# Feed-forward products of an encoder layer as seven block products, in two passes

## The chip, the core and the metric

One core of a Trainium2 chip runs the kernel. The metric is the device time of one execution in microseconds. The kernel before takes 2031.93 us, the median of three runs (2030.33 to 2033.82).

## What is computed

One layer of a streaming encoder in float32, on 1024 prompt tokens and 32 sample tokens (T = 1056 tokens together, width 1024): two recurrent mixers, a projection, cross-attention over a memory, a feed-forward part, a final normalisation. The change lies in the feed-forward part:

```python
D_FF = 2816
...
n = rmsnorm(x, lw['norm_ffn'])
x = x + (jax.nn.silu(n @ lw['w_ff1']) * (n @ lw['w_ff3'])) @ lw['w_ff2']
...
y = rmsnorm(x, norm_final)
```

## The kernel before

**Recording and order.** The network is not issued as it is written. Every call of an engine becomes a node of a graph; `Graph.order` then places the nodes engine by engine with a price for each operation (`price`, L209), gives each tile a place in SBUF or a PSUM bank for as long as its nodes need it, and `Graph.emit` issues them in that order. The line that all instructions carry in the profile is that of `emit` (L337). Each engine works its queue in the order so fixed; all DMAs go through SyncE's queue. `nc.bias` shifts a node's urgency, `nc.phase` and `LEAD` say from when nodes of a later part may be placed, `FIFO` limits how many tiles of a class live at once, and `HOME` says in which region of SBUF a class may lie (`REGIONS`, in units of 66 words of a partition; `f0` has 192 of them).

**Matrix products.** A float32 operand is split into two float32r parts, high and low: ScalarE casts (`CAST`), VectorE or GpSimd subtracts. A product is then three matmuls, high by high, high by low and low by high. `load_w` (L718) loads a column tile of a weight, 128 columns, multiplies it by the norm's gain on VectorE and splits it. `gemm` (L732) goes over three blocks of 352 tokens; the weights are the stationary operand:

```python
for t0, n in blocks:
    ps = self.psg.tile([128, 512], F32, tag="g", name="ps_g")[:, :n]
    for i, k in enumerate(ks or range(nk)):
        ...
        nc.tensor.matmul(ps, lhsT=hi[:, k], rhs=ah, start=i == 0, stop=False)
        ...
        nc.tensor.matmul(ps, lhsT=hi[:, k], rhs=al, start=False, stop=False)
        nc.tensor.matmul(ps, lhsT=lo[:, k], rhs=ah, start=False, stop=i == nk - 1)
    evac(t0, n, ps)
```

**The feed-forward part** (`ffn`, L993). `x` stays in SBUF in its two parts (`xh`, `xl`) and is the moving operand as it is; the factor 1/rms of each token (`rb`, from `rstd`, L884) is multiplied in when a product is taken out of PSUM, so the first products need no `rb`. `hidden(m)` makes one tile of 128 inner features (22 in all): eight input tiles by three blocks for `w_ff1`, the same for `w_ff3`, then sigmoid and products, and the split. After 6, 6, 6, 2 and 2 such tiles (`FF_GROUPS`) `ff2` multiplies that group by its rows of `w_ff2` and adds into the accumulators `acc`, so the inner activations never leave SBUF. The last group goes by blocks of 512, 288 and 256 tokens (`LAST`), so that `final` (transposes on TensorE, squares on ScalarE, `rstd_pow` on GpSimd, a scaling on VectorE, the store) can begin on the first tokens while the last are multiplied.

That is 4752 matmuls of the feed-forward part: 3168 for `w_ff1` and `w_ff3` and 1440 for `w_ff2`, all of 352 tokens, and 48 each of 512, 288 and 256.

**The step ahead of it.** `w_co` of the cross-attention is the last product before the feed-forward part. `residual` (L862) takes it out of PSUM: two additions on VectorE, a cast on ScalarE and a subtraction on GpSimd for the new `x`, and its squares (ScalarE, GpSimd), from which `rstd` gets `rb` over a ones-matmul, Ln, Exp and a Newton step on VectorE.

## Time and profile before

| | |
|---|---|
| median of three runs | 2031.93 us |
| profiled execution: span from first to last instruction | 2034.7 us (no other time is listed for it) |
| TensorE matmuls busy | 1954.2 us, 96% of the span |
| VectorE, ScalarE, GpSimd busy | 1101.1, 801.0, 622.5 us |
| DMA | 100.59 MB, mean 49 GB/s |
| mean granted TensorE clock | 0.978 |

The profile is one execution. PE is TensorE's matmuls, PEld its weight loads (they overlap), DVE is VectorE, ACT ScalarE, POOL GpSimd, SP SyncE. In a group's row stand the engine, the operation, written and read tiles, the shape, the count, then the busy time in us and the mean of one in ns, then idle time ahead of it and what ended that. In a row of the timeline stand the start in us, the length in us, engine, operation, tiles, shape and count; neighbours of one kind are merged. Tiles bear the names of their SBUF regions (`f`, `r`, `mb`, `ma`, `wr`) or `bank` for PSUM. A row of the windows has for each engine the busy time in the stretch, then the granted clock, the DMA engines' busy share and GB/s.

### The profile page before, as it was taken

How to read it: one execution, taken by the hardware profiler on the slowest of the kernel's cores; microseconds unless marked ns; L12 is line 12 of the kernel's file. 1: busy time of each engine (PE TensorE's matmuls, PEld its weight loads, DVE VectorE, ACT ScalarE, POOL GpSimd, SP SyncE). 2: the span in 40 equal slices, each digit the busy share in tenths (PEclk: the TensorE clock that was granted, in tenths of full speed). 3: DMA queues.
4: the chain of work that ended last, by engine and by line, in shares of the span. 5: the costliest groups of instructions: out<-in, count | busy, mean ns of one | idle time of the engine just before them, and what ended most of it. 6: DMA issues, size and time to landing. Idle time of an engine off the chain costs nothing.

```text
span 2034.7 us, 36538 instructions
## 1 busy us (share of the span) xinstructions
PE 1954.2 (96%) x14417; PEld 1813.2 (89%) x14417; DVE 1101.1 (54%) x2584; ACT 801.0 (39%) x2066; POOL 622.5 (31%) x954
## 2 busy tenths in 40 slices
PE   7989999998999899899999999999999999999998
PEld 6878777787877788899989999999999999999997
DVE  4876677768767766635754356333333344323345
ACT  4576546845765676633332233121111112111122
POOL 4742343334434331206300056230022233310221
PEclk8999999998999999899999999999999999999999
DMA  4100100011010101541211111111211111111112
GB/s 139 42 22 25 35 23 27 23 34 33 22 32 18 33 23 58 179 147 42 73 42 42 42 53 42 42 40 40 59 50 39 40 58 42 50 40 53 46 42 86
DMA packets 159115, 100.59 MB, mean 49 GB/s; under 512 B 7776, under 2 KB 153824, under 8 KB 158944
## 3 DMA queue, kind: packets, MB, share of 16 engines
q1 hardware_dynamic: 158944, 98.26, 16.0%
q8 instruction: 113, 1.85, 0.4%
q14 instruction: 58, 0.48, 0.1%
HBM read 86.69 MB, written 11.55 MB: 48 GB/s over the span
## 4 chain that ended last, share of the span: by engine, by line
PE 59%; DVE 4%; POOL 1%; ACT 1%; issue 1%; DMA 1%; SPq 0%; DVEq 0%; ACTq 0%
PE bank L337 59%; DVE f L337 2%; ACT f L337 1%; POOL f L337 1%; DVE r L337 1%; POOL r L337 1%; DVE mb L337 0%; ACT mb L337 0%; DMA wr<-in_w_ck_dram 0%; ACT r L337 0%; DMA f<-mix_scratch 0%; DMA wr<-in_w_cq_dram 0%; DVE wr L337 0%; SPq L337 0%; POOL mb L337 0%
## 5 line engine op out<-in xcount | busy, mean ns | idle before, releaser
L337 PE MATMUL bank<-r 128*128 128x352 f32 x5904 | 1040.1, 331 | 12.4 <-POOL r L337 5.3
L337 PEld LDWEIGHTS bank<-r 128*128 128x128 f32 x5904 | 955.1, 190 | 27.6 <-POOL r L337 5.8
L337 DVE TENSOR_TENSOR f<-bank,f 128x256 f16<-128x256 f32 (+9 forms) x689 | 252.6, 391 | 355.4 <-PE bank L337 339.8
L337 PE MATMUL bank<-mb,r 128*128 128x352 f32 (+3 forms) x2448 | 411.5, 325 | 4.6 <-DVE r L337 2.5
L337 PEld LDWEIGHTS bank<-mb,r 128*128 128x128 f32 x2448 | 396.1, 188 | 9.5 <-DVE r L337 4.3
L337 POOL TENSOR_TENSOR f<-f 128x352 f32<-128x352 f32 (+6 forms) x242 | 198.2, 835 | 482.0 <-ACT f L337 459.4
L337 PE MATMUL bank<-f 128*128 128x64 f16 (+7 forms) x2612 | 291.6, 253 | 35.2 <-DVE f L337 15.7
L337 ACT CAST r<-wr 128x1024 fp32r<-128x1024 f32 (+2 forms) x154 | 145.1, 946 | 311.8 <-PE bank L337 298.1
L337 ACT ACTIVATE f<-f 128x256 f32<-128x256 f32 (+5 forms) x372 | 147.0, 411 | 245.9 <-DVE f L337 217.7
L337 PEld LDWEIGHTS bank<-f 128*128 128x128 f32 (+4 forms) x1564 | 163.6, 162 | 66.8 <-DVE f L337 16.9
L337 ACT COPY f<-f 64x256 f16<-64x256 f16 (+1 forms) x408 | 149.1, 367 | 46.1 <-DVE f L337 37.8
L337 DVE TENSOR_TENSOR r<-wr,r 128x1024 fp32r<-128x1024 f32 (+2 forms) x124 | 142.1, 1150 | 43.5 <-ACT r L337 43.3
L337 DVE TENSOR_TENSOR wr<-wr,f 128x1024 f32<-128x1024 f32 x82 | 105.8, 1292 | 104.5 <-DMA wr<-in_w_ff_dram 89.1
L337 POOL TENSOR_TENSOR r<-f,r 128x352 fp32r<-128x352 f32 x48 | 62.3, 1312 | 271.1 <-DVE f L337 216.9
L337 POOL TENSOR_SCALAR f<-f 128x64 f32<-128x64 f32 (+6 forms) x124 | 54.7, 442 | 159.2 <-DVE f L337 100.0
L337 DVE TENSOR_TENSOR ma<-bank,ma 128x352 f32<-128x352 f32 (+6 forms) x96 | 45.3, 486 | 94.6 <-PE bank L337 84.1
L337 PEld LDWEIGHTS <-f 128*128 128x128 f16 x1156 | 52.5, 99 | 35.6 <-issue 8.2
L337 POOL TENSOR_TENSOR r<-wr,r 128x1024 fp32r<-128x1024 f32 x30 | 71.7, 2393 | 29.5 <-ACT r L337 25.9
L337 ACT CAST mb<-f 128x352 fp32r<-128x352 f32 x66 | 30.9, 484 | 123.0 <-DVE f L337 114.7
L337 PE MATMUL bank<-f,mb 64*64 64x64 f32 (+7 forms) x830 | 75.3, 250 | 1.4 <-DVE f L337 1.1
L337 ACT ACTIVATE f<-bank,f 128x256 f32<-128x256 f32 (+4 forms) x122 | 51.1, 432 | 56.4 <-DVE f L337 19.7
L337 DVE TENSOR_TENSOR f<-bank,r 128x352 f32<-128x352 f32 x60 | 30.4, 518 | 77.0 <-PE bank L337 77.0
(167 smaller groups left out, 1770.6 us busy)
## 6 DMA issues: line engine op xcount, KB each, us to landing
wr<-in_w_ff_dram SPq DMA_DIRECT2D x44, 512.0 KB
wr<-in_w_in_dram SPq DMA_DIRECT2D x30, 512.0 KB
wr<-in_w_ff_dram SPq DMA_DIRECT2D x24, 384.0 KB
f<-mix_scratch SPq DMA_DIRECT2D x24, 176.0 KB
mb<-in_x_prompt_dram SPq DMA_DIRECT2D x16, 256.0 KB
wr<-in_w_ck_dram SPq DMA_DIRECT2D x8, 512.0 KB
wr<-in_w_cv_dram SPq DMA_DIRECT2D x8, 512.0 KB
wr<-in_w_out_dram SPq DMA_DIRECT2D x8, 512.0 KB
```

The source lines that it names most:

```text
L337: getattr(eng, method)(*args, **kw)
```

## The change

Inputs, weights and tokens are cut in halves, and each product of 2x2 blocks is made of seven block products (Strassen's scheme in Winograd's form) instead of eight. A weight block is 256 by 256 (`fast_w`): four 128 by 128 quarters, of which seven stationary operands are formed with four sums on GpSimd, each cast and subtracted. A block of tokens is split in halves of 264 (`TQ`, twice, as two sets), so that a moving operand has 264 columns. `fast` runs the seven products of one column block; products that share a sum stay in one PSUM bank, and the rest of the sums are made when a bank is read.

Before the products the moving side needs its own sums: `ff_hidden` scales `x` by gain and `rb` (16 operations of 528 elements on VectorE), makes 28 operands (seven for each of four pairs of input tiles) with 16 more sums and splits each of them (28 casts, 28 subtractions). `x` itself is written to DRAM (`x_scratch`) by `residual` and no longer split. For every 256 inner features `ff_hidden` makes SiLU, products and the sums of the next stage and writes seven blocks to DRAM (`h_scratch`). Then `ff_out` reads `x` and these blocks back, splits them (28 loads of 264 KB for a group of four), and multiplies in groups of 4, 4, 2 and 1 pairs. The last group goes by sets: `final` runs tiles 0 to 3 after the first and 4 to 8 after the second. The split operands of either pass live in one class of 56 tiles (`op`), the raw blocks in `f0` (`hst2`, at most five). The constants that last share one tile (`lasting`).

The diff, cut to its core; comments were also taken out all over the file.

```diff
-LAST = [(256, 512), (768, 288), (0, 256)]
+TQ = T // 4
...
-FF_GROUPS = (6, 6, 6, 2, 2)
+FF_GROUPS = (4, 4, 2, 1)
...
+LEAD = {0: BIG, 1: 1100, 2: 250, 3: 400, 4: 300, 5: 200, 6: 400}
+HOME = {"keep": ("f0", "r0"), "wr": ("wr",), "wh": ("r0",), "wl": ("r0",), "op": ("r0", "mb"), "sr": ("wr", "ma"),
+        "sh": ("r0", "mb"), "sl": ("r0", "mb"), "sr1": ("wr", "ma"), "sh1": ("r0", "mb"), "sl1": ("r0", "mb"), "sx": ("ma",), "ac": ("f0",), "hst2": ("f0",)}
+FIFO = {"wr": 2, "wh": 2, "wl": 2, "p": 44, "h": 12, "rp": 5, "op": 56, "sr": 2, "sh": 4, "sl": 4, "sr1": 4, "sh1": 28, "sl1": 28, "hst2": 5, "sx": 4, "ckv": 7, "mrow": 2}
...
+        self.lasting = k.tile([128, 480], F32, name="lasting")
+        ident = self.ident = self.lasting[:, 0:128]
...
+        x_dram = nc.real.dram_tensor("x_scratch", [128, KD, T], F32, kind="Internal").ap()
+        self.x_dram = nc.tile([128, KD, T], F32, "x_dram", fixed=x_dram)
...
-        self.ffn()
+        hidden = self.ff_hidden()
+        nc.phase = 5
+        self.ff_out(hidden)
...
+    def residual(self, m, sq, x=None):
+        nc = self.nc
+        def evac(t0, n, ps):
+            hs, ls = self.xh[:, m, t0:t0 + n], self.xl[:, m, t0:t0 + n]
+            t = self.rp("res") if x is None else x[:, t0:t0 + n]
+            nc.vector.tensor_tensor(t, ps, hs.bitcast(F32), ALU.add)
+            nc.vector.tensor_tensor(t, t, ls.bitcast(F32), ALU.add)
+            if x is None:
+                nc.scalar.copy(hs, t)
+                nc.gpsimd.tensor_tensor(ls, t, hs.bitcast(F32), ALU.subtract)
+            else:
+                nc.sync.dma_start(self.x_dram[:, m, t0:t0 + n], t)
+            self.squares(m, sq[:, t0:t0 + n], t, x is not None)
+        return evac
+    def squares(self, m, dst, t, keep=False):
+        nc = self.nc
+        if m == 0:
+            nc.scalar.activation(dst, t, AF.Square)
+        else:
+            q = self.rp("sqr") if keep else t
+            nc.scalar.activation(q, t, AF.Square)
+            nc.gpsimd.tensor_tensor(dst, dst, q, ALU.add)
...
+        self.xf = []
+        for m in range(KD):
+            w = self.load_w(self.i["w_co"][0, :, 128 * m:128 * m + 128], KD)
+            self.xf.append(self.ap.tile([128, T], F32, name="xf"))
+            self.gemm(w, act, KD, self.residual(m, sq, self.xf[m]))
...
+    def halves(self, ap):
+        v = ap.rearrange("p (s h u) -> p s h u", s=2, h=2)
+        return v[:, :, 0], v[:, :, 1]
+    def fast_w(self, ap, nk, tags=("sr", "sh", "sl")):
+        nc = self.nc
+        V, S, G = nc.vector, nc.scalar, nc.gpsimd
+        raw = self.wp.tile([128, nk, 2, 256], F32, tag=tags[0], name="fraw")
+        nc.sync.dma_start(raw, ap.rearrange("(k e p) m -> p k e m", e=2, p=128))
+        a11, a21, a12, a22 = raw[:, :, 0, 0:128], raw[:, :, 0, 128:256], raw[:, :, 1, 0:128], raw[:, :, 1, 128:256]
+        def parts(src):
+            hi, lo = (self.wp.tile([128, nk, 128], F32R, tag=tag, name="f" + tag) for tag in tags[1:])
+            S.copy(hi, src)
+            V.tensor_tensor(lo, src, hi.bitcast(F32), ALU.subtract)
+            return hi, lo
+        yield parts(a11)
+        yield parts(a12)
+        s1, s2 = (self.ap.tile([128, nk, 128], F32, tag="sx", name=t) for t in ("s1", "s2"))
+        G.tensor_tensor(s1, a21, a22, ALU.add)
+        G.tensor_tensor(s2, s1, a11, ALU.subtract)
+        yield parts(s2)
+        G.tensor_tensor(a21, a11, a21, ALU.subtract)
+        yield parts(a21)
+        yield parts(s1)
+        yield parts(a22)
+        G.tensor_tensor(a12, a12, s2, ALU.subtract)
+        yield parts(a12)
+    def fast(self, ws, act, nk, evac, sets=(0, 1)):
+        nc = self.nc
+        ps = {}
+        step = 0.37 * nk * len(sets)
+        ws = iter(ws)
+        for i in range(7):
+            nc.bias = self.turn
+            self.turn += step
+            hi, lo = next(ws)
+            bank = (0, 0, 1, 2, 3, 2, 3)[i]
+            fresh = i in (0, 2, 3, 4)
+            for s in sets:
+                if fresh:
+                    ps[bank, s] = self.psg.tile([128, TQ], F32, tag="g", name="ps_f")
+                p = ps[bank, s]
+                for k in range(nk):
+                    if k % CUT == 0:
+                        nc.cut()
+                    ah, al = act(i, k, 0, s), act(i, k, 1, s)
+                    nc.tensor.matmul(p, lhsT=hi[:, k], rhs=ah, start=fresh and k == 0, stop=False, skip_group_check=True)
+                    nc.tensor.matmul(p, lhsT=hi[:, k], rhs=al, start=False, stop=False, skip_group_check=True)
+                    nc.tensor.matmul(p, lhsT=lo[:, k], rhs=ah, start=False, stop=k == nk - 1, skip_group_check=True)
+                evac(i, s, p)
+    def ff_hidden(self):
+        nc = self.nc
+        V, S, G = nc.vector, nc.scalar, nc.gpsimd
+        ops = [[None] * 4 for _ in range(7)]
+        def parts(src, eng):
+            hi, lo = (self.ap.tile([128, 2, TQ], F32R, tag="op", name=t) for t in ("fh", "fl"))
+            S.copy(hi, src)
+            eng.tensor_tensor(lo, src, hi.bitcast(F32), ALU.subtract)
+            return hi, lo
+        self.turn = 0.0
+        rb = self.halves(self.rb)
+        for h in range(2):
+            for e in range(2):
+                nc.bias = (0.0, 3.0, 6.0, 6.0)[2 * h + e]
+                for k in range(4):
+                    x = self.halves(self.xf[2 * k + e])[h]
+                    V.scalar_tensor_tensor(x, x, self.P("g_ffn", 2 * k + e), rb[h], ALU.mult, ALU.mult)
+                    if h == 0:
+                        ops[e][k] = parts(x, G if e and k % 2 else V)
+        for k in range(4):
+            nc.bias = 6.0
+            (b11, b12), (b21, b22) = (self.halves(self.xf[2 * k + e]) for e in range(2))
+            t1, t2 = (self.ap.tile([128, 2, TQ], F32, tag="ft", name=t) for t in ("t1", "t2"))
+            G.tensor_tensor(t1, b12, b11, ALU.subtract)
+            V.tensor_tensor(t2, b22, t1, ALU.subtract)
+            ops[2][k] = parts(t2, V)
+            nc.bias = 9.0
+            G.tensor_tensor(b12, b22, b12, ALU.subtract)
+            ops[3][k] = parts(b12, V)
+            nc.bias = 12.0
+            ops[4][k] = parts(t1, V)
+            nc.bias = 15.0
+            G.tensor_tensor(b21, b21, t2, ALU.subtract)
+            ops[5][k] = parts(b21, V)
+            nc.bias = 18.0
+            ops[6][k] = parts(b22, G)
+        def act(i, k, lo, s):
+            return ops[i][k][lo][:, s]
+        dram = []
+        for m in range(DFF // 256):
+            d = nc.real.dram_tensor(f"h_scratch{m}", [128, 2, 7, TQ], F32, kind="Internal").ap()
+            dram.append(nc.tile([128, 2, 7, TQ], F32, f"h_dram{m}", fixed=d))
+            cs = slice(256 * m, 256 * m + 256)
+            t = [self.ap.tile([128, 4, TQ], F32, tag="ft4", name="t") for _ in range(2)]
+            v = [None, None]
+            u = [None, None]
+            def sums(i, s, ps, out, first):
+                if i == 0:
+                    u[s] = self.ap.tile([128, TQ], F32, tag="fu", name="fu")
+                    S.copy(u[s], ps)
+                elif i == 1:
+                    first(out[:, 0], ps)
+                elif i == 2:
+                    V.tensor_tensor(u[s], ps, u[s], ALU.add)
+                elif i == 3:
+                    V.tensor_tensor(out[:, 2], ps, u[s], ALU.add)
+                elif i == 4:
+                    V.tensor_tensor(out[:, 2], ps, out[:, 2], ALU.add)
+                else:
+                    o = out[:, 1 if i == 5 else 3]
+                    V.tensor_tensor(o, ps, u[s], ALU.add)
+            def evac1(i, s, ps):
+                sums(i, s, ps, t[s], S.copy)
+                if i == 6:
+                    sg = self.ap.tile([128, 4, TQ], F32, tag="fsg", name="sg")
+                    S.activation(sg, t[s], AF.Sigmoid)
+                    G.tensor_tensor(t[s], t[s], sg, ALU.mult)
+            def evac3(i, s, ps):
+                if i == 0:
+                    v[s] = self.ap.tile([128, 4, TQ], F32, tag="ft4", name="v")
+                sums(i, s, ps, v[s], lambda out, ps: V.tensor_tensor(out, ps, t[s][:, 0], ALU.mult))
+                if i == 6:
+                    x, y = v[s], self.ap.tile([128, 4, TQ], F32, tag="ft4", name="ht")
+                    V.tensor_tensor(x[:, 1:4], x[:, 1:4], t[s][:, 1:4], ALU.mult)
+                    d = dram[m][:, s]
+                    G.tensor_tensor(y[:, 2], x[:, 3], x[:, 0], ALU.subtract)
+                    G.tensor_tensor(y[:, 0], x[:, 2], y[:, 2], ALU.subtract)
+                    G.tensor_tensor(y[:, 1], x[:, 2], x[:, 3], ALU.subtract)
+                    G.tensor_tensor(y[:, 3], x[:, 1], y[:, 0], ALU.subtract)
+                    nc.sync.dma_start(d[:, 0:3], x[:, 0:3])
+                    nc.sync.dma_start(d[:, 3:7], y)
+            self.fast(self.fast_w(self.i["w_ff1"][0, :, cs], 4), act, 4, evac1)
+            self.fast(self.fast_w(self.i["w_ff3"][0, :, cs], 4), act, 4, evac3)
+        return dram
+    def ff_out(self, hidden):
+        nc = self.nc
+        V, S, G = nc.vector, nc.scalar, nc.gpsimd
+        fp = self.ap
+        acc = [fp.tile([128, T], F32, tag="ac", name="acc") for _ in range(KD)]
+        for m in range(KD):
+            nc.sync.dma_start(acc[m], self.x_dram[:, m])
+        common = [fp.tile([128, 2, TQ], F32, tag="ac", name="common") for _ in range(KD // 2)]
+        place = (0, 1, 3, 4, 5, 6, 2)
+        def operands(ms):
+            ops = []
+            for i in range(7):
+                ops.append([])
+                nc.bias = self.turn + 0.74 * len(ms) * i
+                for k, m in enumerate(ms):
+                    raw = fp.tile([128, 2, TQ], F32, tag="hst2", name="hraw")
+                    nc.sync.dma_start(raw, hidden[m][:, :, place[i]])
+                    hi, lo = (fp.tile([128, 2, TQ], F32R, tag="op", name=t) for t in ("fh", "fl"))
+                    S.copy(hi, raw)
+                    (V if k % 2 else G).tensor_tensor(lo, raw, hi.bitcast(F32), ALU.subtract)
+                    ops[i].append((hi, lo))
+            return lambda i, k, lo, s: ops[i][k][lo][:, s]
+        def evac(g, j, i, s, ps):
+            c = [[h[:, s] for h in self.halves(acc[2 * j + e])] for e in range(2)]
+            u = common[j][:, s]
+            def add(dst):
+                V.tensor_tensor(dst, ps, dst, ALU.add)
+            if i == 0 and g == 0:
+                S.copy(u, ps)
+            elif i in (0, 2):
+                add(u)
+            else:
+                add({1: c[0][0], 3: c[1][1], 4: c[1][1], 5: c[1][0], 6: c[0][1]}[i])
+            if i == 6 and g == len(FF_GROUPS) - 1:
+                for n, dst in enumerate((c[1][1], c[1][0], c[0][1])):
+                    (V if n == 2 else G).tensor_tensor(dst, dst, u, ALU.add)
+        at = 0
+        for g, n in enumerate(FF_GROUPS):
+            rows = slice(256 * at, 256 * (at + n))
+            def weights(j, *tags):
+                return self.fast_w(self.i["w_ff2"][0, rows, 256 * j:256 * j + 256], n, *tags)
+            if g < len(FF_GROUPS) - 1:
+                act = operands(range(at, at + n))
+                for j in range(4):
+                    self.fast(weights(j), act, n, partial(evac, g, j))
+            else:
+                nc.phase = 6
+                act = operands(range(at, at + n))
+                ws = [list(weights(j, ("sr1", "sh1", "sl1"))) for j in range(4)]
+                gf = fp.tile([128, D], F32, name="gfin")
+                nc.sync.dma_start(gf, self.i["norm_final"].rearrange("(a d) -> a d", a=1).to_broadcast([128, D]))
+                for s in range(2):
+                    for j in range(4):
+                        self.fast(ws[j], act, n, partial(evac, g, j), sets=(s,))
+                    self.final(acc, gf, fp, range(4 * s, 4 + 5 * s))
+            at += n
...
-    def final(self, acc, gf, fp):
+    def final(self, acc, gf, fp, tiles):
-        for t0 in [128 * i for b, w in LAST for i in range(b // 128, -(-(b + w) // 128))]:
+        for t0 in [128 * i for i in tiles]:
```

84 lines of the change are left out of this document (8 added, 76 removed).

## The prediction

> **What bounds the kernel now.** I read the page's header first, then the windows of the feed-forward part, then its matmuls grouped by shape.
>
> ```profile
> span 2034.7 us, 36538 instructions
> ...
> PE 1954.2 (96%) x14417; PEld 1813.2 (89%) x14417; DVE 1101.1 (54%) x2584; ACT 801.0 (39%) x2066; POOL 622.5 (31%) x954
> ```
>
> ```profile
> 1300.00:1400.00 100.00, 100.00 (x623) 100.00 (x622) 33.67 (x50) 18.25 (x32) 26.05 (x24) 1.00 0.15 43
> ...
> 2000.00:2035.00 35.00, 26.35 (x187) 23.28 (x185) 20.82 (x38) 11.25 (x36) 8.25 (x27) 0.91 0.33 124
> ```
>
> In the middle of the part TensorE has no gap at all at a granted clock of 1.00; DVE is busy a third of the time, POOL a quarter, DMA 15%. Only TensorE's own time can be cut there, and there is room beside it. The end (2000 to 2035 us) is another stage: TensorE is idle for a quarter of it. The matmuls of the part, from its first to its last product:
>
> ```profile
> L337 PE MATMUL bank<-r 128*128 128x352 f32 x3168 | 510.3, 323 | 0.0
> L337 PE MATMUL bank<-mb,r 128*128 128x352 f32 x1440 | 234.4, 324 | 0.0
> L337 PE MATMUL bank<-mb,r 128*128 128x512 f32 x48 | 11.5, 396 | 0.0
> L337 PE MATMUL bank<-mb,r 128*128 128x288 f32 x48 | 7.0, 299 | 0.0
> L337 PE MATMUL bank<-mb,r 128*128 128x256 f32 x48 | 6.4, 286 | 0.0
> ```
>
> Together 769.6 us for 4752 matmuls; one of 352 tokens takes 510.3 / 3168 = 0.161 us. And the border to the step ahead:
>
> ```profile
> 1246.57 5.92 PE L337 MATMUL bank<-r 128*128 128x352 f32 x36
> 1253.28 2.63 PE L337 MATMUL bank<-f 128*128 128x352 f32 x6 [0.79 <-POOL f L337]
> 1255.48 44.80 PE L337 MATMUL bank<-r 128*128 128x352 f32 x276
> ```
>
> The feed-forward matmuls begin at 1246.6 us, before the ones-matmuls of `rstd` (1253.3): they don't need `rb`. From there to the end are 2034.7 - 1246.6 = 788.1 us, of which 788.1 - 769.6 = 18.5 us are not products (`rstd`, transposes, the tail). The sum below replaces these 788.1 us. It is made against the profiled span; that lies 2.8 us above the median 2031.93, so the difference is put on the median.
>
> **Products.** The build order of the changed kernel has 5544 matmuls of 264 columns in place of the 4752: 7/8 of the columns, but a sixth more instructions, so the fixed cost of one matters. The nearest form with a steady stream is 256 columns, in the memory's keys and values:
>
> ```profile
> 813.45 4.51 PE L337 MATMUL bank<-r,ma 128*128 128x256 f32 x36
> 817.79 0.38 PE L337 MATMUL bank<-f 128*128 128x128 f32 x2
> ```
>
> 36 start within 817.79 - 813.45 = 4.34 us, 0.1206 each. Between 0.1206 at 256 and 0.161 at 352 lie 0.42 ns a column, so 264 cost 0.124, and 5544 x 0.124 = 687.5 us: 82 us less than 769.6. Everything else is loss, and what decides is whether it stays below 788.1 - 687.5 = 100.6 us. `rstd`'s ones-matmuls stay: 2.6.
>
> **The start of the first pass.** Now the first operand needs `rb`, and nothing else is left for TensorE. From the last `w_co` product: eviction and addition on DVE, square on ACT, add on POOL, two ones-matmuls (0.88), a DVE step, Ln and Exp, three DVE steps:
>
> ```profile
> L337 DVE SCALAR_TENSOR_TENSOR f<-f 128x352 f32<-128x352 f32 x6 | 2.9, 521 | 0.1
> L337 ACT ACTIVATE f<-f 128x352 f32<-128x352 f32 x76 | 37.0, 496 | 194.8 <-DVE f L337 184.9 <-POOL r L337 9.9
> ```
>
> Six DVE steps at 0.52, three on ACT at 0.50, 0.94 on POOL, 0.88 are 6.4; with some 0.25 at each change of engine about 8 us. Then the operands. In the build order DVE has 43 operations of 528 (or 512) elements ahead of the first eviction, that of the third product, and the sixth product must wait for such evictions; so TensorE does five products (5 x 24 x 0.124 = 14.9 us) and stands. POOL has 18 sums and subtractions of 528 in the same stretch. How the two get on is seen where `residual` and a weight's split meet:
>
> ```profile
> 905.37 0.53 DVE L337 TENSOR_TENSOR f<-f,r 128x352 f32<-128x352 f32 x1
> ...
> 915.78 1.22 DVE L337 TENSOR_TENSOR r<-wr,r 128x1024 fp32r<-128x1024 f32 x1
> ...
> 919.79 4.04 POOL L337 TENSOR_TENSOR r<-f,r 128x352 fp32r<-128x352 f32 x3 [0.25 <-ACT r L337]
> 919.86 1.97 DVE L337 TENSOR_TENSOR r<-wr,r 128x1024 fp32r<-128x1024 f32 x1
> 921.75 1.27 DVE L337 TENSOR_TENSOR f<-f,r 128x352 f32<-128x352 f32 x1
> ...
> 922.94 0.51 DVE L337 TENSOR_TENSOR f<-bank,r 128x352 f32<-128x352 f32 x1
> ...
> 927.07 0.94 POOL L337 TENSOR_TENSOR r<-f,r 128x352 fp32r<-128x352 f32 x1
> ```
>
> Alone: DVE 0.53 for 352 elements and 1.22 for 1024, POOL 0.94. Together: 1.97, 1.27 and 4.04 for three. The five operations alone add up to 4.57, and they took 4.04: these engines take turns, with 0.88 of the sum. By rows DVE needs 43 x 0.71 = 30.5 us (0.71 between 0.53 and 1.22 by size), POOL 18 x 1.35 = 24.3; taking turns (30.5 + 24.3) x 0.88 = 48, side by side 30.5. I take 48, since all these DVE operations read two SBUF tiles as those in the rows do. The stall is 8 + 48 + 1.5 (evictions) - 14.9 = 43 us; bounds 25 and 50. The Trainium skill ("SBUF — State Buffer", section "SBUF: two separate sides") speaks against this change: a VectorE operation with two SBUF inputs and a GpSimd one share a port pair under an exclusive lock, the loser blocked for the whole instruction. By it the preparation would take the full 54.8 us, and the sum would be 7 us higher; the rows agree but for the 0.88.
>
> **Inside the passes.** For 256 inner features TensorE needs 336 x 0.124 = 41.7 us. DVE has 22 PSUM reads of 264, 14 weight splits of 512 and two products of 792: by the rows above and below 9 + 10 + 2 = 21 us; POOL 8 sums of 512, two of 1056, eight of 264, about 24 by 0.94 for 352. Both fit, also by turns (the PSUM read at 922.94 took 0.51 under POOL's three), so I add 4 us only, for PSUM banks that are read while the next product waits; bounds 0 and 35. DMA moves 4 MB in 41.7 us, under the peak:
>
> ```profile
> 4.00:8.00 4.00, 1.00 1.07 355
> ...
> 883.88 11.68 SPq L337 DMA_DIRECT2D f<-mix_scratch x12
> ```
>
> **Changes of operands.** All 56 `op` tiles are in use, so a new group's operand i comes when the last column block is done with the old one: six products (17.9 us) before the end for the first, and the last is needed 17.9 us after it. That covers 35.8 us. The second row: 12 loads of 176 KB go out in 11.68 us through five slots (`rp`), a turn of 4.9 us for load, cast and subtraction. The new loads are 264 KB with a split of 528; about 6 us a turn. In `f0` three slots are left once accumulators, sums and constants lie there (192 - 168 units, 8 each): 2 us a load, 25 x 2 = 50 us against 35.8, 14 to 16 us of stall from group 4 to group 4. From the first pass to the second five slots are free, 28 x 1.2 = 34: covered but for the traffic of `x`, 8 us. Into the groups of 2 and 1: nothing. Bounds of the two together 0 and 45; I take 24.
>
> **The last two groups and the tail.** TensorE needs 504 x 0.124 = 62.5 us, DVE has 112 evictions and 49 weight splits (21 of 256 columns, and 28 of 128 at some 0.28, an estimate below the 0.42 of 256), 8 sums, and 8 scalings for the first tiles:
>
> ```profile
> L337 DVE TENSOR_TENSOR ma<-bank,ma 128x256 f32<-128x256 f32 x4 | 1.5, 421 | 2.2 <-PE bank L337 2.2
> L337 DVE TENSOR_TENSOR r<-wr,r 128x256 fp32r<-128x256 f32 x16 | 6.2, 422 | 0.0
> L337 DVE SCALAR_TENSOR_TENSOR f<-bank,f 128x512 f32<-128x512 f32 x16 | 10.8, 745 | 3.0 <-POOL f L337 3.0
> L337 ACT ACTIVATE f<-bank 128x512 f32<-128x512 f32 x16 | 9.4, 593 | 38.1 <-PE bank L337 29.8 <-DVE ma L337 5.4 <-issue 2.9
> ...
> 2023.41 1.68 PE L337 MATMUL bank<-mb,r 128*128 128x256 f32 x12
> ```
>
> That is 47 + 17 + 3.5 + 6 = 73 us: DVE sets the pace here, with the waits for banks some 80, 18 more than the products. The tail was 2034.7 - 2025.1 = 9.6 us with two tiles left to scale; now it is five, six more squares on ACT at 0.59, each with a reading of its sum, and the scalings behind them: some 5 more, 15.
>
> **Sum.** 687.5 + 2.6 + 43 + 4 + 24 + 18 + 15 = 794 against 788.1: +6, so 2038 us. The mixers are ordered anew because constants share a tile; a wash, give or take 5. Nothing under 0.2% (4 us) can be told from no change.
>
> **Rivals.** *The refills are hidden*: at the two changes of operands a load turns in less than 1.3 us, so the 24 us go: 2014. For it: the trace's peak of 355 GB/s; against it the three slots. *The evictions fall behind in the first pass*: DVE's splits wait for POOL and hold the PSUM reads queued behind them, in 22 column blocks, 1.5 us each: 33 us more, 2071. It decides once a DVE split waits over 1.3 us on average, since then DVE's 21 us become 41.7; the row with 1.97 for 1.22 shows 0.75. *Shorter products don't get cheaper*: by the 288 and 256 groups above (0.146, 0.133) 264 cost 0.136, 66 us more, 2104; those groups hold waits for DVE, the steady row says 0.1206. The Trainium skill ("TensorE: Matmul & The Clock Gate", section "Back-to-back issue gap") has 81 ns for 128 and 131 ns for 512 columns in a stream with weight loads, by whose straight line (an estimate) the products would rise by 24 us instead of falling by 82; the row of 512 (11.5 us for 48) disagrees.
>
> **Numbers.** Forecast 0.42, with a range of its own from 2018 to 2058; refills hidden 0.28; evictions behind 0.25; short products 0.05. The range 1998 to 2078 leaves out the short products, the far end of the second rival and hidden refills that meet a start without turns (25 in place of 43: 1996). Faster: 0.13 + 0.25 = 0.38; same: 0.07 + 0.03 = 0.10; slower: 0.22 + 0.25 + 0.05 = 0.52.
>
> **What would show it.** 264-column matmuls near 0.124 us in 100% busy windows; one idle stretch of TensorE of some 40 us in pieces after `w_co`, ended by DVE; idle at the two changes, ended by ACT casts that wait for DMA. Gaps all through the first pass, or a start under 25 us, would prove me wrong.

## The result, and the profile after

The changed kernel takes 2068.73 us, the median of four runs (2068.06 to 2069.37), beside 2032.79 us (2030.33 to 2033.82) for the kernel before on the same chip: 36 us more, a ratio of 1.0181 with a 95% interval from 1.0166 to 1.0195. The forecast was 2038, with a range from 1998 to 2078. The head of the page of the changed kernel:

```profile
span 2067.3 us, 39611 instructions
...
PE 1900.9 (92%) x15209; PEld 1747.9 (85%) x15209; DVE 1346.7 (65%) x2969; ACT 911.9 (44%) x2293; POOL 869.9 (42%) x1111
```

TensorE has 53 us less to do (1954.2 before), and the span is 33 us longer. Where the time went is read first at the border: the timeline of TensorE of the changed kernel, around the last product of `w_co`.

```profile
1277.98 5.97 PE L338 MATMUL bank<-ma,r 128*128 128x352 f32 x36
1285.71 0.86 PE L338 MATMUL bank<-f 128*128 128x352 f32 x2 [1.75 <-POOL f L338]
1288.10 2.71 PE L338 MATMUL bank<-f 128*128 128x352 f32 x4 [1.53 <-POOL f L338]
1300.97 0.59 PE L338 MATMUL bank<-r,mb 128*128 128x264 f32 x1 [10.16 <-ACT r L338]
```

`w_co` ends at 1277.98 + 5.97 = 1283.9 us, where it ended at 1246.6 before. So the feed-forward part takes 2067.3 - 1283.9 = 783.4 us after 788.1, **4.7 us less**, and everything ahead of it takes **37 us more**, though not one line of the mixers' arithmetic is changed. The loads of `w_out`, the projection behind the mixers, stand in the rows of its tile, of before and then of the changed kernel (eight loads, issue to landing in the order shortest, median, longest, then the times of the first and the last):

```profile
L337 SPq DMA_DIRECT2D wr<-in_w_out_dram x8: 368/390/557, 873.8 to 942.3; - x8
```

```profile
L338 SPq DMA_DIRECT2D wr<-in_w_out_dram x8: 367/390/391, 910.8 to 977.3; - x8
```

The first is 37 us late already, so the loss lies ahead of 911 us, in the mixers. What TensorE does there is seen in the windows (for each engine busy time and count, then granted clock, DMA share, GB/s), of before and of the changed kernel's mixer order (that of the first run below, which shares it):

```profile
400.00:500.00 100.00, 93.16 (x787) 78.02 (x787) 74.14 (x205) 52.45 (x159) 45.95 (x87) 0.95 0.09 28
500.00:600.00 100.00, 95.71 (x983) 80.98 (x982) 71.20 (x219) 71.01 (x199) 35.33 (x67) 1.00 0.09 27
```

```profile
400.00:500.00 100.00, 87.15 (x635) 73.30 (x635) 64.22 (x167) 43.48 (x129) 41.68 (x79) 0.90 0.11 33
500.00:600.00 100.00, 92.47 (x986) 78.38 (x985) 70.40 (x201) 67.05 (x175) 30.37 (x50) 0.95 0.08 22
```

No engine is busier there than before; all of them wait more.

The feed-forward part itself is close to its forecast. Its start, its first pass and its second pass in the windows of the changed kernel:

```profile
1300.00:1350.00 50.00, 24.72 (x107) 21.59 (x108) 48.80 (x49) 19.25 (x36) 32.23 (x18) 0.64 0.00 1
...
1400.00:1450.00 50.00, 50.00 (x413) 50.00 (x412) 33.98 (x44) 16.47 (x30) 30.99 (x22) 1.00 0.24 81
...
1800.00:1850.00 50.00, 43.48 (x324) 41.51 (x324) 32.79 (x46) 15.27 (x27) 31.13 (x22) 0.93 0.53 172
```

At 100% busy and a clock of 1.00, 50 us hold 412 matmuls of 264 columns (the mean of the windows from 1400 to 1700), 0.1214 us each. (From start to start over these 300 us it is 0.1217; a window also counts matmuls that its edges cut. The difference is 2 us over all products.) By that the 5544 need 673 us, and 110 us of the 783 are loss. Counting TensorE's matmuls from the end of `w_co` gives the time of each section and, with 0.1214 us a matmul taken off, its loss:

| section | matmuls | us | loss | forecast |
|---|---|---|---|---|
| start, to the first 264 products | 264 | 85.8 | 53.7 | 45.6 |
| rest of the first pass | 3432 | 420.1 | 3.5 | 4 |
| second pass, first group of 4 | 672 | 99.3 | 17.7 | 8 |
| second group of 4 | 672 | 87.4 | 5.8 | 16 |
| group of 2 | 336 | 46.0 | 5.2 | 33 with the next row |
| group of 1 and the tail | 168 | 44.8 | 24.4 | |

The losses add up to 110, where the forecast had 107. (The two profiled spans are 33 us apart, 37 - 4.7; the medians 36.)

### The profile page after: what moved, and what is told of

Same layout as the page of the kernel before. It is cut to its first block, busy times and chain, and to the rows that moved or that the text cites. A ratio compares the mean times of both kernels' runs of the same rounds, so it can differ in the third digit from the quotient of the medians.

```text
span 2067.3 us, 39611 instructions
## 1 busy us (share of the span) xinstructions
PE 1900.9 (92%) x15209; PEld 1747.9 (85%) x15209; DVE 1346.7 (65%) x2969; ACT 911.9 (44%) x2293; POOL 869.9 (42%) x1111
## 4 chain that ended last, share of the span: by engine, by line
PE 57%; DVE 11%; ACT 4%; POOL 4%; issue 4%; DMA 2%; DVEq 0%; SPq 0%; POOLq 0%; ACTq 0%
PE bank L338 57%; DVE f L338 6%; DVE r L338 3%; ACT f L338 3%; POOL f L338 2%; DVE mb L338 1%; DMA f<-h_scratch 1%; POOL ma L338 1%; DVE ma L338 1%; POOL mb L338 1%; ACT mb L338 1%; POOL r L338 1%; ACT r L338 0%; DMA wr<-in_w_cv_dram 0%; ACT ma L338 0%
## 5 line engine op out<-in xcount | busy, mean ns | idle before, releaser
L338 PE MATMUL bank<-r 128*128 128x352 f32 (+1 forms) x5322 | 978.9, 314 | 44.1 <-ACT r L338 10.4
L338 DVE TENSOR_TENSOR f<-bank,f 128x264 f32<-128x264 f32 (+8 forms) x951 | 343.5, 384 | 242.7 <-PE bank L338 227.4
L338 PE MATMUL bank<-mb,r 128*128 128x264 f32 (+1 forms) x2430 | 445.1, 302 | 12.4 <-DVE mb L338 5.4
L338 PE MATMUL bank<-f 128*128 128x64 f16 (+5 forms) x2725 | 305.0, 256 | 48.7 <-DVE f L338 25.7
L338 POOL TENSOR_TENSOR f<-f 128x264 f32<-128x264 f32 (+11 forms) x231 | 208.4, 911 | 303.3 <-ACT f L338 243.7
L338 PEld LDWEIGHTS bank<-f 128*128 128x128 f32 (+3 forms) x1667 | 172.2, 162 | 78.7 <-DVE f L338 22.1
L338 PE MATMUL bank<-r,mb 128*128 128x264 f32 x870 | 198.8, 291 | 14.2 <-ACT r L338 10.2
L338 ACT ACTIVATE f<-f 128x256 f32<-128x256 f32 (+7 forms) x351 | 143.8, 425 | 134.6 <-DVE f L338 112.4
L338 PE MATMUL bank<-mb 128*128 128x264 f32 (+3 forms) x1116 | 175.8, 280 | 11.4 <-DVE mb L338 9.7
L338 PEld LDWEIGHTS bank<-r,mb 128*128 128x128 f32 x870 | 147.2, 194 | 17.3 <-ACT r L338 11.6
L338 POOL TENSOR_TENSOR ma<-ma 128x512 f32<-128x512 f32 (+4 forms) x81 | 97.9, 1214 | 102.6 <-DVE mb L338 44.8
```

The source lines that it names most:

```text
L338: getattr(eng, method)(*args, **kw)
```

## The experiments

**Theory A** says that the 36 us are the mixers' new order, which follows from the constants' shared tile; **rival B**, that the feed-forward part, its regions and its limits cost them. Two runs tell them apart from both ends. (The runs stand beside the kernel before on three chips: 2032.33 us for it with runs one to four, 2032.81 with five to eight, 2029.11 with nine and ten. Across chips the ratios to it count.) The first is the kernel before with the shared tile:

```diff
-        ident = self.ident = k.tile([128, 128], F32, name="ident")
+        self.lasting = k.tile([128, 480], F32, name="lasting")
+        ident = self.ident = self.lasting[:, 0:128]
...
-        self.ones = k.tile([128, 128], F32, name="ones")
+        self.ones = self.lasting[:, 128:256]
```

and so for `nhalf`, `par` and `dpar`. As in the changed kernel, the constant `eps_rms`, which nothing reads, is left out as well.

> The kernel before with one edit: the constants ident, ones, nhalf, par and dpar become parts of one tile `lasting`, as in the changed kernel; the feed-forward part is left as it was before. In the build order this alone puts the mixers' instructions in the changed kernel's order (TensorE's rows 434 to 4165). Theory A (the 36 us are lost ahead of the feed-forward part, because the constants' shared tile reorders the mixers): 2033 + 37 = 2070 us, range 2063 to 2075, with the first w_out load at about 911 us instead of 874. Rival B (the feed-forward part itself, or the new regions and limits, cost the 36 us): 2033 us within 5.

It took 2070.35 us (2069.73 to 2071.06), a ratio of 1.0186 to before with an interval from 1.0166 to 1.0206: the whole loss, with the feed-forward part untouched. The missing `eps_rms` is not the cause: when the kernel before is planned without it, the order of every engine stays as it was. The run's rows for `w_out` and for the first feed-forward products:

```profile
L337 SPq DMA_DIRECT2D wr<-in_w_out_dram x8: 367/391/391, 911.3 to 977.3; - x8
```

```profile
1279.85 5.92 PE L337 MATMUL bank<-r 128*128 128x352 f32 x36
```

From 1279.85 to its end at 2068.5 are 788.7 us, the 788.1 of before. Rival B falls.

The second run comes from the other end: the changed kernel with constants of their own, of which three are copied to a small tile ahead of `w_co`, so that the first tiles can be given up.

```diff
+        late = self.cp.tile([128, 480], F32, name="late")
+        V.tensor_copy(late[:, 0:128], self.ident)
+        V.tensor_copy(late[:, 128:144], self.nhalf)
+        V.tensor_copy(late[:, 144:152], self.P("g_ffn", 0, KD))
```

> The changed kernel with the constants in tiles of their own as before; a small copy of ident, nhalf and the gains is made just ahead of w_co, so that the first tiles can be given up for the feed-forward part. The mixers then stand in the order of the kernel before (TensorE's rows up to 4153). Theory A: the feed-forward part keeps the 783.5 us of the changed kernel's trace (788.1 before), so 2032.8 - 4.6 = 2028 us, range 2022 to 2036. Rival B: 2069 us as the changed kernel.

It took 2043.76 us (2037.86 to 2045.52): 25 of the 36 us are back, 16 us short of what theory A wanted and outside its range. The first `w_out` load is at 863.4 us and `w_co` ends at 1239.9, but the feed-forward part takes 795.3 us in the profile. The excess over the changed kernel sits in the second pass: 103.2, 92.2 and 52.7 us for its first three groups in place of 99.3, 87.4 and 46.0. So A holds for the mixers. The rest is put down to the new tile, which runs five and six take up.

**Theory C** is that VectorE and GpSimd take turns, and that work given to GpSimd therefore doesn't relieve VectorE; **rival D**, that they work side by side. The third run issues the 18 GpSimd operations of the start on VectorE; order and places stay those of the second run.

```diff
-                eng = getattr(real, node.eng)
+                eng = getattr(real, "vector" if node.tag and node.eng == "gpsimd" else node.eng)
...
+        nc.tag = "start"
```

> The kernel of the run before, in the same order and places, with the 18 sums and subtractions that GpSimd makes for the operands at the start of the first pass issued on VectorE instead. Theory C (VectorE and GpSimd take turns when both read two SBUF tiles, so GpSimd's work there buys nothing and its slower operations cost): VectorE does them in 18 x 0.7 = 12.6 us in place of GpSimd's 24, so the start is 6 to 9 us shorter than in the run before. Rival D (they work side by side and the long VectorE durations have another cause): VectorE's queue gets 12 us longer and so does the time.

It took 2031.34 us (2027.03 to 2041.86), 12.4 less than the second run; in the profiles the start went from 85.6 to 76.7 us. VectorE's groups from 1250 to 1300 us, of the second run and then of the third:

```profile
L338 DVE SCALAR_TENSOR_TENSOR f<-f 128x528 f32<-128x528 f32 x16 | 15.4, 1026 | 0.0
L338 DVE TENSOR_TENSOR r<-f,r 128x528 fp32r<-128x528 f32 x12 | 13.5, 1161 | 0.0
```

```profile
L338 DVE SCALAR_TENSOR_TENSOR f<-f 128x528 f32<-128x528 f32 x16 | 11.4, 766 | 0.0
L338 DVE TENSOR_TENSOR f<-f 128x528 f32<-128x528 f32 x16 | 10.9, 705 | 0.0
L338 DVE TENSOR_TENSOR r<-f,r 128x528 fp32r<-128x528 f32 x15 | 10.1, 703 | 0.0
```

VectorE took on more operations and each became shorter (1161 to 703 ns). Rival D, by which the time had to rise by 12 us, falls.

The fourth run does the same for the subtractions of the refilled operands.

```diff
+                    nc.tag = "refill"
                     (V if k % 2 else G).tensor_tensor(lo, raw, hi.bitcast(F32), ALU.subtract)
+                    nc.tag = None
```

> The kernel of the run before, and besides the subtractions of the refilled operands of the second pass, every other of which was on GpSimd, all on VectorE. Theory C: each GpSimd subtraction of 528 holds VectorE up for longer than the 0.7 us that it takes there, so a turn of the refill gets shorter and the changes of operands (28.8 us lost in the second pass) give back some 5 us each, 5 to 10 us in all. Rival E (the refill's turns are set by its loads: ScalarE's casts waited 38.7 us for DMA): no change within 2 us. Rival D: 3 to 6 us slower.

It took 2021.30 us (2019.99 to 2022.29), 10 less again, as C had it. In the profiles the first group of the second pass went from 104.0 to 99.0 us and the group of 2 from 51.3 to 43.9. Rivals D and E fall.

**Theory S** is that the slots for the raw operands (`hst2`) set the turn of a refill. In the plan of SBUF, which is worked out when the kernel is built, the second run's `late` lies across the middle of a page of `f0`, and the groups of 2 and 1 are left with two slots; the changed kernel has three there. In the second group of 4, too, the plan puts 26 of the 28 raw operands in two slots, and in three with the smaller tile. The fifth run cuts the tile in the second run's kernel:

```diff
-        late = self.cp.tile([128, 480], F32, name="late")
+        late = self.cp.tile([128, 152], F32, name="late")
```

> The second run's kernel (the change with the mixers in the order of before) with the small late tile cut from 480 to 152 words. In the plan of SBUF of the second run that tile lies across the middle of a page of `f0`, so that only two slots are left for the raw operands of the groups of 2 and 1, where the changed kernel has three; with 152 words three are left again. Theory S (slots set the turn of a refill): the second pass is back at the changed kernel's length, 11.7 us shorter than in the second run, 2043.8 - 11.7 = 2032 us, range 2026 to 2037. Rival T (the turn is set by the subtractions alone): 2044 us within 3.

It took 2033.87 us (2030.52 to 2038.46), 9.9 less. SyncE's loads for the second group of 4, the first and the last row of 26 loads, of the second run and then of the fifth:

```profile
1824.66 9.89 SPq L338 DMA_DIRECT2D f<-h_scratch  x4
...
1889.78 9.77 SPq L338 DMA_DIRECT2D f<-h_scratch  x4
```

```profile
1826.41 12.29 SPq L338 DMA_DIRECT2D f<-h_scratch  x5
...
1882.03 2.61 SPq L338 DMA_DIRECT2D f<-h_scratch  x3
```

The 26 loads go out in 1899.55 - 1824.66 = 74.9 us with the second run's slots and in 1884.64 - 1826.41 = 58.2 with the fifth's. The groups of the second pass take 99.3, 88.1 and 45.7 us, the changed kernel's 99.3, 87.4 and 46.0: the second run's excess there is explained. Not all of it is gained: the rest of the first pass takes 424.5 us after 419.0 in the profiles, with TensorE standing 4.39 us up to 1743.2, shortly before its end. Theory S holds, and with it theory A: with the old order of the mixers and equal slots, the changed kernel is within 0.2% of the kernel before (1.0007, from 0.9996 to 1.0018). The sixth run is the same cut in the fourth run's kernel.

> The fourth run's kernel (start and refills on VectorE) with the same cut of the late tile, so three slots in place of two in the groups of 2 and 1. Theory S: part of the 11.7 us is already paid back by the quicker subtractions (51.3 to 43.9 us in the group of 2), so 4 to 8 us less than the fourth run: 2013 to 2017 us. Rival T: 2021 us within 3.

It took 2016.66 us (2014.06 to 2019.28), 4.6 less than the fourth.

**Theory Q** looks for the loss at the change from the first pass to the second in SyncE's queue. In the fourth run four loads go out right behind the last two stores of the first pass, which wait for GpSimd's sums, and TensorE stands; SyncE's and TensorE's timeline:

```profile
1754.41 1.48 SPq L338 DMA_DIRECT2D h_scratch<-ma  x2
1756.00 2.76 SPq L338 DMA_DIRECT2D f<-h_scratch  x4
```

```profile
1760.38 0.59 PE L338 MATMUL bank<-r 128*128 128x264 f32 x1 [4.25 <-ACT r L338]
...
1763.57 2.65 PE L338 MATMUL bank<-r 128*128 128x264 f32 x13
1767.29 0.51 PE L338 MATMUL bank<-r 128*128 128x264 f32 x2 [1.06 <-ACT r L338]
1768.53 0.39 PE L338 MATMUL bank<-r,mb 128*128 128x264 f32 x1 [0.73 <-DVE mb L338]
...
1769.86 0.65 PE L338 MATMUL bank<-r 128*128 128x264 f32 x2
1770.30 0.42 PE L338 MATMUL bank<-r,mb 128*128 128x264 f32 x1
...
1780.57 3.32 PE L338 MATMUL bank<-r,mb 128*128 128x264 f32 x26
```

The seventh run gives the stores to GpSimd's queue.

```diff
+                    nc.tag = "store"
                     nc.sync.dma_start(d[:, 0:3], x[:, 0:3])
                     nc.sync.dma_start(d[:, 3:7], y)
+                    nc.tag = None
```

and the line that picks the engine takes GpSimd for that tag.

> The kernel of the run before, with the stores of the inner activations issued from GpSimd's queue in place of SyncE's. Theory Q (SyncE's queue is in order, and the loads of the second pass stand behind the last stores, which wait for GpSimd's sums): in the fourth run four loads left at 1756.0 us right after the stores of 1754.4, TensorE stood 4.25 us and then went on at 0.22 us a product matmul instead of 0.12 for some 12 us; that goes in part, 4 to 9 us less than the run before. Rival R (the loads wait for free slots anyway): no change within 2 us. Rival U (issuing from GpSimd's queue holds up its sums): 3 us or more slower.

It took 2021.79 us (2020.49 to 2023.87), 5.1 more than the sixth. The first group of the second pass takes 96.5 us, 95.5 in the sixth run, so the order of that queue is not what it waits for, at least with these slots. The first pass loses instead; a window of it:

```profile
1400.00:1450.00 50.00, 49.66 (x408) 49.48 (x407) 35.59 (x49) 14.28 (x25) 26.65 (x24) 1.00 0.30 102
```

408 matmuls in place of 412, and the rest of the first pass takes 428.7 us, 423.0 in the sixth run. Rival U has the sign right, but it isn't GpSimd's sums that are held up. VectorE's splits of weights are, as its groups from 1350 to 1650 us show, of the sixth run and then of the seventh:

```profile
L338 DVE TENSOR_TENSOR r<-wr,r 128x512 fp32r<-128x512 f32 x22 | 20.4, 928 | 8.1 <-PE bank L338 6.8
```

```profile
L338 DVE TENSOR_TENSOR r<-wr,r 128x512 fp32r<-128x512 f32 x21 | 48.3, 2302 | 8.0 <-PE bank L338 6.8
```

2.30 us in place of 0.93 is a mean of two kinds. Seven of the 21 splits take 4.87 to 5.08 us, one for every 256 inner features, and the other 14 take 0.96 on average. One of the seven, and what GpSimd does meanwhile:

```profile
1462.51 4.89 DVE L338 TENSOR_TENSOR r<-wr,r 128x512 fp32r<-128x512 f32 x1 [0.98 <-PE bank L338]
```

```profile
1462.84 0.75 POOL L338 TENSOR_TENSOR f<-f 128x264 f32<-128x264 f32 x1
...
1464.97 0.56 POOL L338 DMA_DIRECT2D h_scratch<-f  x1
1465.55 1.29 POOL L338 TENSOR_TENSOR ma<-ma 128x512 f32<-128x512 f32 x1
1466.79 0.57 POOL L338 DMA_DIRECT2D h_scratch<-f  x1
```

The split ends with the second store, at 1467.4. GpSimd's sums of 264 take 0.75 us there, without turns, where their groups in the sixth run have a mean of up to 1.29. So VectorE waits for a whole string of sums and stores; which of the two holds it, this trace does not separate.

The eighth run carries theory C on, on top of the sixth run's kernel: the sums of weight quarters of the whole part on VectorE.

```diff
+        nc.tag = "weights"
         G.tensor_tensor(s1, a21, a22, ALU.add)
         G.tensor_tensor(s2, s1, a11, ALU.subtract)
+        nc.tag = None
```

and so around the two other sums.

> The kernel of the run before last (three slots, start and refills on VectorE), and the sums of weight quarters of the whole feed-forward part on VectorE too; GpSimd keeps only the inner activations' products and sums. Theory C (VectorE and GpSimd take turns): GpSimd's 1.5 us sums beside the steps of `rstd` and the first scalings go, and in the last groups, where VectorE sets the pace, each turn lost costs more than the 0.69 us that a sum takes there: 4 to 8 us less. Rival D (side by side): VectorE gets 8 x 0.69 = 5.5 us more for each product of 256 columns that takes 20.8 us, fits in the first pass, and costs in the groups that VectorE paces: 5 to 10 us more.

It took 2014.22 us (2005.44 to 2017.02), 2.4 less than the sixth, with ranges that overlap. Rival D is out again: GpSimd was busy 92 us in the windows from 1240 to 1350 and from 1600 on, 211 in the sixth run, and VectorE took its sums over without a longer time in all. Only in the last two groups, where D put the cost, do the profiles show some: 92.5 us for both after 88.0, against 7.4 less in the rest. But C's 4 to 8 us aren't there either. The start is 74.8 us after 75.2: these sums now stand in VectorE's queue between the steps of `rstd`.

The ninth run asks why the shared tile changes the order: it narrows, in the first run's kernel, the planner's rule for memsets to users of the same columns.

```diff
-                later = [u for b in n.bufs for u in b.users if u.i > n.i and u.calls[0][0] != "memset"]
+                later = [u for b in n.bufs for u in b.users if u.i > n.i and u.calls[0][0] != "memset" and (b.name != "lasting" or near(u, b))]
```

> The first run's kernel (the kernel before with the shared tile `lasting`), with one rule of the planner narrowed: a memset on `lasting` inherits the predecessors of later users of the same columns alone, no longer those of every later user of the tile. This gives the mixers a third order, which leaves that of before and that of the changed kernel at TensorE's row 434. Theory M (the memsets tied together by the shared tile cost the 37 us): back to 2033 us within 6. Rival P (the tile's place and lifetime in `f0` reorder the mixers, and any other order than the one of before is a draw): a time of its own, 8 us or more from 2033, between 2041 and 2085 us.

It took 2078.69 us (2072.52 to 2081.50), a ratio of 1.0244 (1.0227 to 1.0261). Theory M falls. Three orders of the same mixer instructions cost 2033, 2070 and 2079 us. What about the shared tile sets them apart stays open.

The tenth run adds, to the eighth run's kernel, the last pair's sums on VectorE.

```diff
+                    nc.tag = "last" if m == DFF // 256 - 1 else None
                     G.tensor_tensor(y[:, 2], x[:, 3], x[:, 0], ALU.subtract)
```

> The eighth run's kernel (three slots; start, refills and weight sums on VectorE) and the four sums of the last pair of inner activations (two sets, 8 operations of 264) on VectorE as well, so that its stores, and the loads queued behind them, leave earlier at the change from the first to the second pass. Theory Q (that queue sets the change, as far as anything): GpSimd's 8 x 1.2 us become 8 x 0.37 us, 2 to 5 us less than the eighth run: 2009 to 2012 us. Rival R (loads wait for slots, and VectorE's evictions wait behind the added sums): no change within 3 us.

It took 2013.17 us (2012.41 to 2014.19), 1.0 less than the eighth: within rival R, and Q falls a second time. (The eight sums take 0.42 to 0.43 us each on VectorE, not 0.37.) As a ratio to the kernel before it is 0.9917 (0.9902 to 0.9931), after 0.9919 (0.9903 to 0.9934) for the sixth and 0.9898 (0.9867 to 0.9928) for the eighth: these three can't be told apart. They are 0.8 to 1.0% faster than the kernel before, and 52 to 56 us below the changed kernel as it was made.

The sections of the feed-forward part in the profiles, in us:

| run | start | rest of first pass | 4 | 4 | 2 | 1 and tail | part |
|---|---|---|---|---|---|---|---|
| changed kernel | 85.8 | 420.1 | 99.3 | 87.4 | 46.0 | 44.8 | 783.4 |
| 2: old order | 85.6 | 419.0 | 103.2 | 92.2 | 52.7 | 42.6 | 795.3 |
| 3: start on VectorE | 76.7 | 419.4 | 104.0 | 90.9 | 51.3 | 42.6 | 784.9 |
| 4: refills too | 75.1 | 423.0 | 99.0 | 89.7 | 43.9 | 43.1 | 773.8 |
| 5: run 2, three slots | 85.5 | 424.5 | 99.3 | 88.1 | 45.7 | 45.7 | 788.8 |
| 6: run 4, three slots | 75.2 | 423.0 | 95.5 | 86.9 | 42.4 | 45.6 | 768.6 |
| 7: run 6, stores from GpSimd | 75.3 | 428.7 | 96.5 | 85.8 | 42.4 | 43.9 | 772.6 |
| 8: run 6, weight sums too | 74.8 | 421.7 | 92.0 | 84.7 | 46.3 | 46.2 | 765.6 |
| 10: last sums too | 73.3 | 421.1 | 93.0 | 84.9 | 46.3 | 44.0 | 762.6 |

These are single profiled executions: a difference of 1 or 2 us between two rows says little. Ahead of the part they differ more: with one and the same mixer order `w_co` ends between 1239.9 and 1248.5 us. In the second, the sixth and the seventh run the profiled execution is also the fastest of the run.

## Why the prediction was right or wrong

The time lies inside the range, on the side that was given 0.52, and that is luck. The 6 us of loss were to come from the feed-forward part, which in the profiles got 4.7 us shorter; the whole loss came from the mixers. With their old order and three slots (fifth run) the change is worth nothing that can be told from zero. The 2068.73 us also lie near the 2071 of the rival in which the evictions fall behind, whose mechanism did not occur.

**The step that failed** is "The mixers are ordered anew because constants share a tile; a wash, give or take 5". It was +37 us. The prediction had seen that the order changes, gave the change no rows, and took a new order from a greedy planner for a draw around the old one. The first run puts the whole loss on that edit alone, and the ninth shows a third order that is worse still. The two other orders at hand cost 38 and 50 us, each against the kernel before on its chip, where the bound was 5; and the new order runs from row 434 of TensorE's build order to row 4165, as the first run's expectation has it, so through most of the mixers. Why these orders are slower stays open.

**Products**: forecast 687.5 us by 0.124 each, measured 673 by 0.1214. The line through the steady rows of 256 and 352 columns was 2% high. The rival by which shorter products don't get cheaper (0.136) is out.

**Start**: forecast 45.6 us with `rstd`, lost 53.7. The mechanism was right, and one size was off, the lead. It was put at 8 us from rows in which each VectorE step of `rstd` takes 0.52; in the changed kernel the first scaling starts at 1299.48, 15.6 us after `w_co`. GpSimd's weight sums run beside these steps:

```profile
1293.41 4.54 POOL L338 TENSOR_TENSOR ma<-ma 128x512 f32<-128x512 f32 x3
...
1293.86 2.97 DVE L338 SCALAR_TENSOR_TENSOR f<-f 128x352 f32<-128x352 f32 x2
```

That is 1.49 a step. (Moved to VectorE in the eighth run, these sums stand in its own queue, and the start is only 0.4 us shorter than in the sixth.) The preparation, forecast at 48 us by turns, took 47.4, from the first scaling to the first eviction:

```profile
1299.48 2.81 DVE L338 SCALAR_TENSOR_TENSOR f<-f 128x528 f32<-128x528 f32 x4
...
1346.90 0.42 DVE L338 TENSOR_TENSOR f<-bank,f 128x264 f32<-128x264 f32 x1
```

The turns show in the same operation of VectorE with GpSimd at work and without, and in GpSimd's own with VectorE's two-tile operations out of the way:

```profile
1317.13 8.63 POOL L338 TENSOR_TENSOR f<-f 128x528 f32<-128x528 f32 x5
1319.39 1.80 DVE L338 TENSOR_TENSOR f<-f 128x528 f32<-128x528 f32 x1
...
1324.54 1.80 DVE L338 TENSOR_TENSOR r<-f,r 128x528 fp32r<-128x528 f32 x1
...
1327.47 0.69 DVE L338 TENSOR_TENSOR r<-f,r 128x528 fp32r<-128x528 f32 x1
```

```profile
1347.84 1.31 POOL L338 TENSOR_TENSOR r<-f,mb 128x528 fp32r<-128x528 f32 x1 [3.91 <-PE bank L338]
```

0.69 us alone, 1.80 beside GpSimd, whose five operations take 1.73 each: both engines end one operation every 1.73 us or so, one after the other. Alone the pair adds up to 0.69 + 1.31 = 2.00, so the factor is 0.87, where the prediction had 0.88. The rule of the Trainium skill ("SBUF — State Buffer", section "SBUF: two separate sides") that was weighed there, an exclusive lock held for a whole instruction, agrees with the turns and with the third run. The full sum that was worked out from it, 54.8 us, was not reached.

**Inside the first pass**: forecast 4, lost 3.5, and the windows are 100% busy. The rival of the evictions that fall behind is out for this kernel; turns are taken there too (the 30 splits of 512 from `ma` between 1400 and 1700 us take 1612 ns each), but VectorE keeps a third of its time free.

**Changes of operands**: forecast 24, lost 23.5 in the two groups of 4, but not where it was put. The first change, taken for nearly covered (8), lost 17.7, and the one from group to group (16) lost 5.8. Slots were the right idea (three as counted; with two, the second run lost 10.6 and 11.9 in the second group of 4 and the group of 2). What the prediction didn't have is the GpSimd subtraction that frees a slot and takes turns with VectorE: with it on VectorE (fourth run) 13 us of the second pass come back. Whether that is the slot freed sooner or VectorE held up less, the runs don't separate. The rival of hidden refills was not reached in any run: with the subtractions on VectorE and three slots (sixth run) the first three groups still lose 13.9, 5.3 and 1.6 us.

**Last groups and tail**: forecast 33 (18 for the groups of 2 and 1, 15 for the tail), lost 5.2 + 24.4 = 29.6. The window of the changed kernel from 2000 us on:

```profile
2000.00:2050.00 50.00, 47.12 (x360) 45.40 (x359) 44.91 (x127) 13.62 (x51) 25.44 (x46) 0.97 0.09 33
```

360 matmuls are done where 412 would fit, and VectorE is busy nine tenths of the time, with some of it spent on turns: it sets the pace as forecast.

So the feed-forward part was forecast to take 794 us and took 783, with errors that partly cancel: 14 too much for the products, 8 too little for the start. The forecast was 31 us low in all because one short sentence, outside the part that was worked out, hid the largest error.

## What to carry to other kernels

Where a planner orders a whole program, a small change of a tile reorders stages that the diff doesn't touch: compare the order of every stage, and give a changed order a price from both sides, or hold it fixed (here a late copy of three constants did). Before work is given to GpSimd to relieve VectorE, look in the trace for the same VectorE operation with GpSimd at work and without: here the 18 operations of the start alone cost 9 us there. And count slots where a transfer has to turn: one slot less in a stage's leftover space cost 10 us.

## What the runs showed of the hardware

A stall can cost TensorE more than its length. The fourth run again, in windows around its wait of 4.25 us (the granted clock is the third number from the end):

```profile
1755.00:1758.00 3.00, 1.13 (x10) 0.91 (x8) 1.39 (x4) 0.00 (x0) 0.55 (x1) 1.00 0.97 360
1759.00:1765.00 6.00, 4.47 (x18) 4.15 (x19) 2.83 (x4) 2.53 (x4) 0.00 (x0) 0.50 1.03 337
1766.00:1769.00 3.00, 1.20 (x7) 0.78 (x7) 2.17 (x3) 2.39 (x5) 2.27 (x2) 1.00 0.84 276
1769.10:1772.00 2.90, 2.90 (x15) 2.90 (x14) 2.90 (x3) 0.32 (x1) 2.90 (x3) 0.50 0.03 10
1772.50:1776.00 3.50, 3.36 (x27) 3.15 (x27) 3.50 (x5) 1.93 (x4) 0.51 (x1) 1.00 0.25 64
```

The clock is halved in two separate stretches. In them matmuls start 0.22 us apart (two within 1770.30 - 1769.86 = 0.44 in the rows of theory Q), between and after them 0.12. The first stretch begins in the wait of 4.25 us. The second comes after 3 us in which TensorE was busy for 1.20, with no wait longer than 1.06 us in the rows. The Trainium skill ("TensorE: Matmul & The Clock Gate", section "Part 1: The HAM clock gate (the "warmup" mystery)") has a gate that halves the clock after an idle window of about 3.4 us. The rate agrees; both falls come after less. The first is there by 1759.0, 2.9 us after the last matmul ended (1760.38 - 4.25 = 1756.13). The forecast priced stalls by their length alone. This one cost some 3 us more in slow matmuls, as an estimate from these windows: 18 and 15 of them take 4.47 + 2.90 us, and 33 x 0.1214 are 4.0.

And stores issued from GpSimd's queue came with longer operations of VectorE: one split of 512 elements in three went from under 1 us to some 5 in the seventh run, until the second store was out. The Trainium skill ("SBUF — State Buffer", section "SBUF: two separate sides") has the other side of it: GpSimd writes such a transfer's descriptors itself, and is locked out of the port pair that it shares with VectorE while VectorE runs an operation in a 2-port mode. Here VectorE's operation is the one that gets longer.
